# A two-layer hybrid trunk: the borders from token mixer to feed-forward reordered, with the first two up-products of eight pairs put ahead

## The chip, the cores and the metric

The kernel runs on one core of a Trainium2 chip. The metric is the device time of one execution in microseconds (us), the median over the runs shown. PE is TensorE, DVE is VectorE, ACT is ScalarE, POOL is GpSimd, and SP is the engine whose queue issues every DMA of this kernel.

## What is computed

Two DeepNorm layers of width 1024 over 1024 tokens, all in float32. Layer 0 mixes tokens by a dilated window attention, layer 1 by a gated linear recurrence (HGRN2); each is followed by a squared-ReLU feed-forward of width 4096.

```python
for i in range(DEPTH):
    j = i // N_MIXERS
    if i % N_MIXERS == 0:
        y = dilated_attention_mixer(x, attn_w_in[j], attn_w_out[j])
    else:
        y = hgrn2_mixer(x, hgrn_w_in[j], hgrn_w_out[j], hgrn_norm_g[j], lbs[i])
    x = layer_norm(DEEPNORM_ALPHA * x + y, ln_mix_g[i], ln_mix_b[i])
    y = squared_relu_mlp(x, ffn_w_up[i], ffn_w_down[i])
    x = layer_norm(DEEPNORM_ALPHA * x + y, ln_ffn_g[i], ln_ffn_b[i])
```

The attention has three head groups (dilations 1, 4, 16) whose outputs are mixed by a softmax over the groups' log sums; a "unit" below is one pair of heads of one group.

## The kernel before

**Precision.** Every large matrix product is made of three matmuls: an operand is split into a high part (ACT rounds it) and a low part (DVE subtracts, line 125 in `split`), and high x high, high x low, low x high are summed in one bank of PSUM. A "split" below is one ACT and one DVE instruction on 128x512 elements.

**SBUF.** Nearly everything lies in one pool of 46 equal slots of 128x1024 (`U`, `NSLOT`). An instruction that writes a new tile waits until a slot is free. PSUM has eight banks: three "mm", two "s", two "pt", one "o".

**Order.** Each engine works through its own list. Inside the attention's product loop PE's and DVE's lists are as written (`in_order`). Elsewhere the framework lays out the lists when the program is built, by the order of writing and its own estimate of what is ready; at run time every list, SP's DMAs too, is strictly in order, and a waiting instruction holds up all behind it.

**Border 1** (attention to feed-forward, about 1006 to 1220 us). The attention's last pair of units is still in its softmax when the loop of input products ends. `attention` returns what is left of it in `fill`, lists of small pieces: the rotary steps (`ra`, `rb`; a DMA fetches the rotated copy, L446), six core steps for each of the two units (`ca`, `cb`: scores L476, exponentials L490, transposes L500, products L515), the statistics of each unit (`sa`, `sb_`: `combine_tr`, a transpose L541, then a DMA to DRAM and back), and the mixing of the groups (`mx`: `combine` on tiny tiles, six DMAs per part into `frow`, then six `fb` products L597 with DVE multiplications L598 to L602). `oN` is the list of attention outputs, eight tiles of 128 features x 1024 tokens; the first six are spilled to DRAM.

`outproj_ln` projects them. `pr.pre`, called at the last input product, loads and splits the first two (`NPRE`) tiles of `oN`, tokens 0 to 511 (h = 0), with their weights. Then the rest up to six (`NKA`) follow, the second halves of the weights, the second token half (h = 1) of all six, and three residual tiles `z`. **Stage A** accumulates these six features for the token tiles 0 to 5 (two column halves each: twelve half-tiles of 18 matmuls, L170 to L172), and between them pops `fill`, one list at a time: five during the first three half-tiles, one after them, and one after each further half-tile. What `fill` still holds then is written out behind all of stage A. **The finish** (`fin`) adds features 6 and 7 for tiles 0 to 5, all eight for tiles 6 and 7, normalises each tile (`ln_math`: DVE, ACT and one POOL addition, L201) and stores it. `tr(t)` transposes a normalised tile (L210, into the two "pt" banks) and makes the operands of the feed-forward's first product by a scheme with seven instead of eight sub-products (`Fast`): for the second token half this makes the sums T1 to T4, by DVE and POOL in scratch tiles `fs`, ten splits' halves in all (L220, L221).

**The feed-forward** has 16 pairs `p`, each of seven products `i` in 1 to 7. Products 1 and 2 need the first token half alone, the others need T1 to T4. So `seq` puts (p, 1) and (p, 2) of the first four pairs (`NAHEAD`) ahead, then their other five products, then the other pairs in full. After each of the first four products one list of `late` is popped: `tr(6)`, `tr(4)`, `tr(7)`, `tr(5)`. Weights are loaded six products ahead (`load_up`), split three ahead (`split_up`). A pair's `upa` tile holds product 1's copy (L1009) and the square of product 2 (L1012), and stays until its other five products are done.

**Border 2** (HGRN2 to feed-forward, about 2208 to 2370 us) uses the same `outproj_ln` with seven features in stage A and six short lists in `fill`.

Of the kernel before, what the change touches and what calls it, by code (L numbers as in the profile page):

```python
# [9 lines left out]
F32 = mybir.dt.float32  # L10
# [23 lines left out]
NPRE = 2  # L34
SPILL = (6, 5)
NKA = (6, 7)
NAHEAD = 4
# [12 lines left out]
def trunk_kernel(  # L50
# [258 lines left out]
    def attention(pre):  # L309
# [413 lines left out]
        for n in range(len(seq)):  # L723
# [8 lines left out]
            if n == len(seq) - 1:  # L732
                pre(oN)
# [44 lines left out]
    class Out:  # L778
# [10 lines left out]

        def split_w(self, k, dm):  # L790
            hi, lo, raw = self.w[k]
            c = slice(dm * 512, dm * 512 + 512)
            nc.sync.dma_start(raw[:, c], self.w_dram[k][:, c])
            split(raw[:, c], hi[:, c], lo[:, c])
            if dm == 1:
                self.w[k] = (hi, lo)

        def load(self, k, oN, h):
            if k >= SPILL[self.mixer]:
                self.raw[k] = oN[k]  # L800
                return
            if h == 0:
                self.raw[k] = U("onr")
            c = slice(h * 512, h * 512 + 512)
            nc.sync.dma_start(self.raw[k][:, c], oN[k][:, c])
# [14 lines left out]
    def outproj_ln(pr, oN, fill, resid, gB_ap, bB_ap, keep):  # L820
# [9 lines left out]
        for k in range(NPRE, nka):  # L830
# [9 lines left out]
        NA = (6, 6)[pr.mixer]  # L840
# [9 lines left out]
        def stage_a(tiles, n):  # L850
            os = [bank("mm", "pmm") for _ in tiles]
            for ks in [range(nka)] if len(tiles) == 1 else [(k,) for k in range(nka)]:
                for (t, dm), o in zip(tiles, os):
                    rows(o, a, w, t, dm, ks, ks[0] == 0, ks[-1] == nka - 1)
                if len(ks) == 1 and ks[0] in pops:
                    for f in fill.pop(0) if fill else []:
                        f()
            for (t, dm), o in zip(tiles, os):
                c = slice(dm * 512, dm * 512 + 512)
                nc.vector.scalar_tensor_tensor(z[t][:, c], z[t][:, c], ALPHA, o, op0=ALU.mult, op1=ALU.add)  # L860
            for _ in range(n):
                for f in fill.pop(0) if fill else []:
                    f()

        pops = (1, 2, 3, 4, 5, 6) if len(fill) > 12 else (2, 4)
        stage_a([(0, 0), (1, 0), (2, 0)], 1)
        for t in range(NA):
            load_z(max(t, 1) + 1)
            if t == NA - 3:
                for k in range(nka, NK):  # L870
                    pr.load_w(k)
                    pr.split_w(k, 1)
            for dm in range(2):
                if t > 2 or dm:
                    stage_a([(t, dm)], 1)
# [3 lines left out]
        load_z(7)  # L879
        for h in range(2):  # L880
            for k in range(nka, NK):
                pr.raw[k] = oN[k]
                split_k(k, h)
        gB = bcast_rows(gB_ap, "gB")
        bB = bcast_rows(bB_ap, "bB")
        xn = Fast(name + "f")
# [4 lines left out]
        def fin(t, dms=(0, 1)):  # L891
            for dm in dms:
                o = bank("mm", "pmm")
                c = slice(dm * 512, dm * 512 + 512)
                if t < NA:
                    rows(o, a, w, t, dm, range(nka, NK), True, True)
                    nc.vector.tensor_add(z[t][:, c], o, z[t][:, c])
                else:
                    rows(o, a, w, t, dm, range(8), True, True)
# [12 lines left out]
        fin(7, (0,))  # L912
        tr(1)
        fin(4)
        tr(2)
        tr(3)
        fin(7, (1,))
        fin(5)
        return xn, [lambda: tr(6), lambda: tr(4), lambda: tr(7), lambda: tr(5)]


    def ffn(li, xf, late, res, gB_ap, bB_ap, last, pre=None):
# [11 lines left out]
        raw, comb, H = {}, {}, {}  # L934

# [36 lines left out]

        st = [{} for _ in range(NP)]
# [24 lines left out]
        def product_up(n):  # L998
# [9 lines left out]
            if i == 1:  # L1008
                act(p1, o, AF.Copy)  # L1009
            elif i == 2:  # L1010
# [223 lines left out]
        for n in range(len(seq)):  # L1234
            load_up(n + LOADUP)
            product_up(n)
            if late:
                late.pop(0)()
# [263 lines left out]
    hds = [dp.tile([7, NFF // 2, P, 512], F32, name=f"hd{i}") for i in range(2)]  # L1502
    x1d = dp.tile([S, D], F32, name="x1d")
# [3 lines left out]
    oN, fill = attention(pr.pre)  # L1507
# [87 lines left out]
```

## Time and profile before

| | us |
|---|---|
| median of 3 runs (2995.59 to 2996.76) | 2995.66 |
| the profiled execution, its own time | 2997.35 |
| span of its trace | 2995.6 |
| PE busy (95% of the span) | 2832.5 |
| DVE busy (70%) | 2085.3 |
| ACT busy (49%) | 1459.9 |
| POOL busy (15%) | 437.3 |

The profiled execution took 1.75 us more than its span, and stands 1.69 us above the median. PE is busy in 95% of the span, and the chain of work that ended last runs over PE for 75% of it. A busy PE is not yet PE at its peak: a matmul of 512 columns counts 0.39 us though the next one starts 0.23 us after it, and at the lower clock the same work counts as busy for longer. So in the tables by stage the number of instructions is to be read with the busy time.

### The profile page before, as it was taken

To read this page: it belongs to the slowest core of one execution; us is meant where nothing else is said; L and a number is where in the kernel's file an instruction comes from. 1 tells how busy PE (TensorE), PEld (TensorE's weight loads), DVE (VectorE), ACT (ScalarE), POOL (GpSimd) and SP (SyncE) were. 2 spreads that over 40 slices of the span, in tenths; PEclk is the share of its full clock that TensorE was granted. 3 is DMA by queue.
4 is the path that set the end of the run, shared out by engine and by line. 5 is a ranking of instruction groups with operands and counts; after the bars stand their busy time and mean duration, and the time that the engine had idled before them with its cause. 6 is when DMAs were issued, how large, how long until landed. Compare 5 with 4: busy or idle time off the path is not lost.

```text
span 2995.6 us, 40619 instructions
## 1 busy us (share of the span) xinstructions
PE 2832.5 (95%) x14152; PEld 2243.5 (75%) x14152; DVE 2085.3 (70%) x3725; ACT 1459.9 (49%) x3136; POOL 437.3 (15%) x211
## 2 busy tenths in 40 slices
PE   7899999999999878999999998999999899999998
PEld 6677777777677656777778876778877677778876
DVE  7668776786787648766686966564566766678784
ACT  5454555555555445444444535554553544454442
POOL 0112111010111103000051311110101200034300
PEclk9999999999999999999999999999999899999999
DMA  8885777767777512344494733101131344475662
GB/s 340 276 268 185 251 250 240 236 239 251 262 234 263 160 55 102 134 151 150 140 316 122 255 118 130 36 29 57 64 134 61 122 146 143 151 272 184 204 204 74
DMA packets 214717, 525.16 MB, mean 175 GB/s; under 512 B 31600, under 2 KB 45936, under 8 KB 214512
## 3 DMA queue, kind: packets, MB, share of 16 engines
q1 hardware_dynamic: 214512, 522.57, 52.0%
q8 instruction: 111, 1.82, 0.3%
q14 instruction: 94, 0.77, 0.1%
HBM read 400.57 MB, written 96.34 MB: 166 GB/s over the span
## 4 chain that ended last, share of the span: by engine, by line
PE 75%; DMA 10%; DVE 10%; issue 2%; ACT 2%; SPq 1%; POOL 0%; DVEq 0%; ACTq 0%; POOLq 0%
PE pmm L638 6%; PE pmm L637 6%; PE pmm L639 6%; PE pup L1004 5%; PE pup L1006 5%; PE pup L1005 5%; PE pdy L1124 4%; PE pdy L1126 4%; PE pdy L1125 4%; PE pmm L158 3%; PE pmm L159 3%; PE pmm L160 3%; DMA wb<-in_w_up_dram 3%; PE pdx L1125 3%; PE pdx L1126 3%
## 5 line engine op out<-in xcount | busy, mean ns | idle before, releaser
L637 PE MATMUL pmm<-xh,H 128*128 128x512 f32 x1008 | 409.9, 407 | 12.8 <-ACT H L410 7.9
L638 PE MATMUL pmm<-xl,H 128*128 128x512 f32 x1008 | 399.3, 396 | 14.0 <-DMA xl<-xtd 13.2
L639 PE MATMUL pmm<-xh,H 128*128 128x512 f32 x1008 | 398.2, 395 | 1.5 <-DVE H L418 1.5
L448 POOL TENSOR_TENSOR rot<-rot,sinT 128x1024 f32<-128x1024 f32 x48 | 136.5, 2845 | 865.7 <-DMA rot<-e 385.2
L638 PEld LDWEIGHTS pmm<-xl,H 128*128 128x128 f32 x1008 | 192.5, 191 | 54.5 <-DMA xl<-xtd 16.4
L637 PEld LDWEIGHTS pmm<-xh,H 128*128 128x128 f32 x1008 | 192.4, 191 | 53.8 <-ACT H L410 7.9
L639 PEld LDWEIGHTS pmm<-xh,H 128*128 128x128 f32 x1008 | 191.9, 190 | 44.1 <-DVE H L418 2.7
L487 DVE CUSTOM_DVE_ANT_0 p<-s,mask 128x128 f32<-128x128 f32 (+1 forms) x384 | 113.1, 347 | 148.2 <-PE s L476 137.2
L1124 PE MATMUL pdy<-dT,dS 128*128 128x512 f32 x512 | 201.7, 394 | 7.5 <-ACT dS L124 7.5
L490 ACT ACTIVATE p<-p,stats 128x128 f32<-128x128 f32 (+1 forms) x384 | 168.2, 441 | 78.4 <-DVE stats L487 78.2
L1125 PE MATMUL pdy<-dT,dS 128*128 128x512 f32 x512 | 201.1, 393 | 0.0
L1126 PE MATMUL pdy<-dT,dS 128*128 128x512 f32 x512 | 201.1, 393 | 0.0
L125 DVE TENSOR_TENSOR dS<-dr,dS 128x512 fp32r<-128x512 f32 x192 | 167.5, 872 | 18.1 <-ACT dS L124 17.4
L124 ACT ACTIVATE dS<-dr 128x512 fp32r<-128x512 f32 x192 | 120.1, 626 | 121.1 <-DVE dT L125 41.8
L503 ACT ACTIVATE pts<-ppt 128x256 f32<-128x256 f32 (+1 forms) x192 | 85.8, 474 | 150.4 <-PE ppt L500 140.4
L158 PE MATMUL pmm<-f0nh,wh 128*128 128x512 f32 x384 | 153.2, 399 | 0.7 <-ACT wh L124 0.7
L160 PE MATMUL pmm<-f0nh,wl 128*128 128x512 f32 x384 | 149.9, 390 | 0.0
L159 PE MATMUL pmm<-f0nl,wh 128*128 128x512 f32 x384 | 149.7, 390 | 0.0
L1096 POOL TENSOR_TENSOR hold<-hold,dr 128x512 f32<-128x512 f32 x32 | 48.3, 1509 | 630.3 <-DMA hold<-in_w_down_dram 325.4
L1124 PEld LDWEIGHTS pdy<-dT,dS 128*128 128x128 f32 x512 | 97.4, 190 | 28.6 <-ACT dS L124 8.3
L125 DVE TENSOR_TENSOR dT<-dr,dT 128x512 fp32r<-128x512 f32 x128 | 116.0, 920 | 4.1 <-ACT dT L124 3.7
L201 POOL TENSOR_TENSOR z<-z,bB 128x1024 f32<-128x1024 f32 x24 | 63.2, 2640 | 357.7 <-ACT z L200 354.7
(394 smaller groups left out, 7233.6 us busy)
## 6 DMA issues: line engine op xcount, KB each, us to landing
xh<-xtd SPq DMA_DIRECT2D x154, 512.0 KB
xl<-xtd SPq DMA_DIRECT2D x154, 512.0 KB
dr<-hd SPq DMA_DIRECT2D x192, 256.0 KB
dr<-in_w_down_dram SPq DMA_DIRECT2D x160, 256.0 KB
rot<-e SPq DMA_DIRECT2D x192, 128.0 KB
wa<-in_w_up_dram SPq DMA_DIRECT2D x40, 512.0 KB
wa<-in_w_attn_dram SPq DMA_DIRECT2D x36, 512.0 KB
wb<-in_w_attn_dram SPq DMA_DIRECT2D x36, 512.0 KB
```

The costliest lines, as they stand in the source:

```text
L125: nc.vector.tensor_sub(lo, raw, hi.bitcast(F32))
L158: nc.tensor.matmul(o, wh[:, k], xs.h(k), start=k == 0, stop=False)
L159: nc.tensor.matmul(o, wh[:, k], xs.l(k), start=False, stop=False)
L160: nc.tensor.matmul(o, wl[:, k], xs.h(k), start=False, stop=k == NK - 1)
L490: act(p[:, h, :n], p[:, h, :n], AF.Exp, bias=sS[:, 0, h, b:b + 1], scale=-1.0, accum_out=sS[:, 1, h, b:b + 1])
L637: nc.tensor.matmul(o, wh, hi[k // 2][:, c], start=begin and k == 0, stop=False, skip_group_check=True)
L638: nc.tensor.matmul(o, wh, lo[k // 2][:, c], start=False, stop=False, skip_group_check=True)
L639: nc.tensor.matmul(o, wl, hi[k // 2][:, c], start=False, stop=end and k == 3, skip_group_check=True)
L1004: nc.tensor.matmul(o, wh, xf.h(b, k), start=begin and k == 0, stop=False, skip_group_check=True)
L1124: nc.tensor.matmul(o[q], h, T_[:, L], start=begin, stop=False, skip_group_check=True)
L1125: nc.tensor.matmul(o[q], h, T_[:, R], start=False, stop=False, skip_group_check=True)
L1126: nc.tensor.matmul(o[q], l, T_[:, L], start=False, stop=end, skip_group_check=True)
```

## The change

- `attention`: `pr.pre_steps` takes the place of `pr.pre`. It issues the loads of three features (`PREA`) nine products before the end, and makes their six splits one by one after each of the last seven products. `fill` has another order (`mine`): single core steps of the two units in turn, the statistics of each unit with its fifth core step, the mixing from the 16th of 22 lists on.
- `outproj_ln`: stage A covers tiles 0 to 3 alone (eight half-tiles); `tick` pops `fill` evenly after every feature of a half-tile; a feature that comes in meanwhile (k = 6) joins stage A; the loads and splits of the second token half (`second`) come two at a time behind the half-tiles, the rest behind stage A. The finish takes tile 0, 4, 1, 4, 2, 5, 3, 5, 6, 6, 7 with all eight features for tiles 4 to 7. `late` has the four transposes in the order 4, 5, 6, 7, each with two empty places before it.
- `ffn`: `NAHEAD` is 8. Pairs 4 to 7 store product 1's copy to DRAM (`p1d`) and load it again, with the square of product 2, when their other products come near.

```diff
+PREA = 3
+EARLY = (2, 0)
+NAHEAD = 8
+NSTAY = 4
+LATE = 2
...
-            if n == len(seq) - 1:
-                pre(oN)
+            if n == len(seq) - 2 * PREA - 3:
+                early = pre(oN)
+            if n >= len(seq) - 2 * PREA - 1:
+                next(early, None)
...
-        lists = [[ra[0]], [rb[0], rb[1]], [ra[1]], [ca[0], rb[2]], [ca[1], cb[0]]]
-        lists = [done[k:k + 1] + (lists[k] if k < len(lists) else []) for k in range(max(len(done), len(lists)))]
-        lists += [[ca[2 + k], cb[1 + k]] for k in range(4)]
-        lists += [[sa[0], cb[5]], [], [sb_[0]], [], [], [mx[0]], [mx[1]], [mx[2]], [], [], mx[3:6], mx[6:9]]
+        mine = [[ra[0]], [rb[0], rb[1]], [ra[1]], [ca[0], rb[2]], [ca[1]], [cb[0]], [ca[2]], [cb[1]], [ca[3]], [cb[2]],
+                [ca[4], sa[0]], [cb[3]], [ca[5]], [cb[4], sb_[0]], [cb[5]], [mx[0]], [mx[1]], [mx[2]], [],
+                mx[3:5], mx[5:7], mx[7:9]]
+        lists = [done[k:k + 1] + (mine[k] if k < len(mine) else []) for k in range(max(len(done), len(mine)))]
...
+        def pre_steps(self, oN):
+            for k in range(PREA):
+                self.load(k, oN, 0)
+                raw = U("wor")
+                self.w[k] = (None, None, raw)
+                nc.sync.dma_start(raw[:, :512], self.w_dram[k][:, :512])
+
+            def steps():
+                for k in range(PREA):
+                    raw = self.w[k][2]
+                    hi, lo = U("woh", F32R), U("wol", F32R)
+                    self.w[k] = hi, lo, raw
+                    split(raw[:, :512], hi[:, :512], lo[:, :512])
+                    yield
+                    self.split_k(k, 0)
+                    yield
...
-        for k in range(nka):
-            pr.load(k, oN, 1)
-            split_k(k, 1)
...
+        ticks = 3 * nka + 5 * 7
+
+        def tick():
+            count[0] += 1
+            while fill and count[1] * ticks < count[0] * total:
+                for f in fill.pop(0):
+                    f()
+                count[1] += 1
...
+        def second(n):
             for _ in range(n):
-                for f in fill.pop(0) if fill else []:
-                    f()
...
+                if ahead and len(oN) > ahead[0]:
+                    k = ahead.pop(0)
+                    pr.load(k, oN, 1)
+                    split_k(k, 1)
+
+        ks = list(range(nka))
+        stage_a([(0, 0), (1, 0), (2, 0)], ks)
+        for n, (t, dm) in enumerate([(0, 1), (1, 1), (2, 1), (3, 0), (3, 1)]):
...
+            stage_a([(t, dm)], ks)
+            if n >= EARLY[pr.mixer]:
+                second(2)
...
         fin(0)
+        fin(4, (0,))
         fin(1)
-        fin(6, (0,))
+        fin(4, (1,))
         fin(2)
-        fin(6, (1,))
+        fin(5, (0,))
         fin(3)
         tr(0)
-        fin(7, (0,))
+        fin(5, (1,))
         tr(1)
-        fin(4)
         tr(2)
+        fin(6, (0,))
         tr(3)
-        fin(7, (1,))
-        fin(5)
-        return xn, [lambda: tr(6), lambda: tr(4), lambda: tr(7), lambda: tr(5)]
+        fin(6, (1,))
+        fin(7)
+        late = []
+        for t in (4, 5, 6, 7):
+            late += [None] * LATE + [lambda t=t: tr(t)]
+        return xn, late
...
+            if i == 6 and NSTAY <= p < NAHEAD:
+                t = st[p]["a"] = U("upa")
+                nc.sync.dma_start(t[:, L], p1d[li, p])
+                nc.sync.dma_start(t[:, R], hd[0, p])
...
             if i == 1:
                 act(p1, o, AF.Copy)
+                if NSTAY <= p < NAHEAD:
+                    nc.sync.dma_start(p1d[li, p], p1)
```

## Rows read from the trace of the kernel before

**Rows 1.** The page's part 2: TensorE's busy tenths and granted clock in 40 slices.

```profile
PE   7899999999999878999999998999999899999998
PEclk9999999999999999999999999999999899999999
```

**Rows 2.** Busy time by stage: stretch, length, then each engine's busy us (instructions), clock, DMA.

```profile
1006.00:1103.00 97.00, 84.80 (x495) 61.29 (x496) 59.02 (x139) 49.38 (x135) 4.75 (x2) 1.00 0.40 128
1103.00:1128.00 25.00, 9.98 (x38) 6.04 (x35) 12.83 (x26) 2.86 (x7) 0.00 (x0) 0.67 0.05 15
1128.00:1170.00 42.00, 40.70 (x195) 32.76 (x195) 38.26 (x78) 20.28 (x47) 14.62 (x6) 0.99 0.26 97
1170.00:1219.00 49.00, 33.52 (x129) 24.78 (x130) 41.12 (x76) 29.99 (x71) 16.00 (x10) 0.86 0.30 106
1219.00:1274.00 55.00, 54.16 (x237) 43.98 (x236) 41.01 (x67) 24.55 (x43) 0.00 (x0) 1.00 0.46 156
2208.00:2279.00 71.00, 70.39 (x370) 57.34 (x369) 35.80 (x72) 22.51 (x45) 0.00 (x0) 1.00 0.25 82
2279.00:2308.00 29.00, 27.78 (x130) 22.48 (x129) 27.47 (x55) 10.58 (x23) 11.18 (x5) 1.00 0.17 65
2308.00:2368.00 60.00, 44.91 (x173) 33.55 (x172) 51.20 (x99) 38.28 (x92) 19.23 (x12) 0.77 0.34 122
```

**Rows 3.** PE in order of time, border 1: start, duration, operation, idle before it.

```profile
1046.94 0.93 PE L476 MATMUL s<-kT,qT 64*128 64x128 f32 x8 [1.67 <-DVE kT L450]
...
1147.31 1.04 PE L210 MATMUL lnpt<-ident,z 128*128 128x128 f32 x8
```

**Rows 4.** All engines in order of time: the last exponential of the attention.

```profile
1092.41 0.50 ACT L490 ACTIVATE p<-p,stats 128x256 f32<-128x256 f32 x1
```

**Rows 5.** PE in order of time, from the statistics to the finish.

```profile
1103.83 0.28 PE L541 MATMUL mpt<-ident,stats 128*32 128x128 f32 x1
...
1119.83 1.19 PE L597 MATMUL fb<-frow,bsel 128*128 128x512 f32 x2 [13.62 <-DMA frow<-fl]
...
1125.41 0.79 PE L170 MATMUL pmm<-woh,aoh 128*128 128x512 f32 x1 [0.47 <-ACT aoh L124]
```

**Rows 6.** SP's DMA issues in order of time, in the attention's tail.

```profile
1024.68 5.51 SPq L845 DMA_DIRECT2D z<-in_x_dram  x3
...
1030.96 5.62 SPq L446 DMA_DIRECT2D rot<-e  x8
```

**Rows 7.** PE's waits, 1170 to 1220: us in total, times, longest.

```profile
PE lnpt L210 <- DVE fs L288: 5.5, 2, 3.6
PE pup L1004 <- ACT H L124: 5.3, 3, 3.4
```

**Rows 8.** PE's waits, 2279 to 2370.

```profile
PE lnpt L210 <- DVE fs L288: 5.1, 2, 3.1
PE pup L1004 <- ACT H L124: 5.0, 2, 3.4
```

**Rows 9.** PE in order of time: matmuls at the lower clock, then at full clock.

```profile
1216.13 0.63 PE L1006 MATMUL pup<-af21h,H 128*128 128x512 f32 x1
1216.55 0.63 PE L1004 MATMUL pup<-af21h,H 128*128 128x512 f32 x1
...
1218.02 0.39 PE L1005 MATMUL pup<-afT2l,H 128*128 128x512 f32 x1
...
1219.60 0.39 PE L1006 MATMUL pup<-afT2h,H 128*128 128x512 f32 x1
```

**Rows 10.** Stage 1170 to 1219, instructions with the scratch tiles fs alone.

```profile
1170.00:1219.00 49.00, 22.56 (x40) 13.46 (x36) 10.78 (x8) 0.86 0.30 106
```

**Rows 11.** DVE's groups, 1170 to 1219: busy us, mean ns.

```profile
L125 DVE TENSOR_TENSOR H<-wa,H 128x512 fp32r<-128x512 f32 x8 | 5.4, 674 | 0.0
```

**Rows 12.** DVE's groups, 2279 to 2368.

```profile
L125 DVE TENSOR_TENSOR H<-wa,H 128x512 fp32r<-128x512 f32 x8 | 7.6, 949 | 0.0
```

More of the change, by code (lines that the diff above doesn't have):

```diff
@@ L788, in load_w @@
             self.split_w(k, 0)
+        def pre_steps(self, oN):
[13 more added lines that the diff above has]
+                    yield
+            return steps()
         def split_w(self, k, dm):
@@ L801, in load @@
                 return
[L802 to L803 removed]
+            self.raw[k] = U("onr")
             c = slice(h * 512, h * 512 + 512)
@@ L829, in outproj_ln @@
         nka = NKA[pr.mixer]
-        for k in range(NPRE, nka):
+        for k in range((PREA, NPRE)[pr.mixer], nka):
             pr.load(k, oN, 0)
@@ L848, in outproj_ln, with stage_a @@
         load_z(2)
-        def stage_a(tiles, n):
+        parts = {}
+        total = max(len(fill), 1)
+        count = [0, 0]
+        ticks = 3 * nka + 5 * 7
[5 more added lines that the diff above has]
+                count[1] += 1
+        def stage_a(tiles, ks):
             os = [bank("mm", "pmm") for _ in tiles]
-            for ks in [range(nka)] if len(tiles) == 1 else [(k,) for k in range(nka)]:
+            for k in ks:
                 for (t, dm), o in zip(tiles, os):
-                    rows(o, a, w, t, dm, ks, ks[0] == 0, ks[-1] == nka - 1)
-                if len(ks) == 1 and ks[0] in pops:
-                    for f in fill.pop(0) if fill else []:
-                        f()
+                    rows(o, a, w, t, dm, (k,), k == ks[0], k == ks[-1])
+                    tick()
             for (t, dm), o in zip(tiles, os):
@@ L860, in stage_a @@
                 nc.vector.scalar_tensor_tensor(z[t][:, c], z[t][:, c], ALPHA, o, op0=ALU.mult, op1=ALU.add)
+                parts[t, dm] = ks
+        ahead = [k for k in range(NK)]
+        def second(n):
             for _ in range(n):
[L862 to L867, printed above, removed]
-            load_z(max(t, 1) + 1)
[L869 to L875, printed above, removed]
+                if ahead and len(oN) > ahead[0]:
[5 more added lines that the diff above has]
+        for n, (t, dm) in enumerate([(0, 1), (1, 1), (2, 1), (3, 0), (3, 1)]):
+            load_z(max(t, 1) + 1)
+            if n in (1, 3) and len(w) < NK:
+                k = len(w)
+                pr.load_w(k)
+                pr.split_w(k, 1)
+            k = len(ks)
+            if k < 7 and len(oN) > k and k < len(w):
+                pr.raw[k] = oN[k]
+                split_k(k, 0)
+                ks = ks + [k]
+            stage_a([(t, dm)], ks)
+            if n >= EARLY[pr.mixer]:
+                second(2)
+        while len(w) < NK:
+            k = len(w)
+            pr.load_w(k)
+            pr.split_w(k, 1)
         while fill:
@@ L878, in outproj_ln @@
                 f()
[L879 to L883, printed above, removed]
+        for k in range(len(ks), NK):
+            pr.raw[k] = oN[k]
+            split_k(k, 0)
         gB = bcast_rows(gB_ap, "gB")
         bB = bcast_rows(bB_ap, "bB")
+        second(NK)
         xn = Fast(name + "f")
@@ L891, in fin @@
         def fin(t, dms=(0, 1)):
+            load_z(t)
             for dm in dms:
@@ L894, in fin @@
                 c = slice(dm * 512, dm * 512 + 512)
-                if t < NA:
-                    rows(o, a, w, t, dm, range(nka, NK), True, True)
+                old = parts.get((t, dm), [])
+                rows(o, a, w, t, dm, [k for k in range(NK) if k not in old], True, True)
+                if old:
                     nc.vector.tensor_add(z[t][:, c], o, z[t][:, c])
                 else:
-                    rows(o, a, w, t, dm, range(8), True, True)
                     nc.vector.scalar_tensor_tensor(z[t][:, c], z[t][:, c], ALPHA, o, op0=ALU.mult, op1=ALU.add)
@@ L934, in ffn @@
         raw, comb, H = {}, {}, {}
+        st = [{} for _ in range(NP)]
         def key(p, half, i):
@@ L971, in split_up @@
             H[p, i] = parts_of(a22 if i == 4 else comb[p][i], "H")
-        st = [{} for _ in range(NP)]
         def pair_tile(p, name):
@@ L1236, in ffn @@
             product_up(n)
-            if late:
-                late.pop(0)()
+            f = late.pop(0) if late else None
+            if f:
+                f()
             split_up(n + SPLITUP)
@@ L1502, in trunk_kernel @@
     hds = [dp.tile([7, NFF // 2, P, 512], F32, name=f"hd{i}") for i in range(2)]
+    p1d = dp.tile([2, NAHEAD, P, 512], F32, name="p1d")
     x1d = dp.tile([S, D], F32, name="x1d")
@@ L1506, in trunk_kernel @@
     pr = Out(w_attn_out, "a", 0)
-    oN, fill = attention(pr.pre)
+    oN, fill = attention(pr.pre_steps)
     xf, late = outproj_ln(pr, oN, fill, lambda t: x[t * P:(t + 1) * P, :],
```

2 lines of the change are left out of this document (removed).

## The prediction

> **What bounds the kernel now.** I read the page's slices first. PE is full nearly everywhere, and apart from the start the slices that fall below 9 lie at two places, around 1000 to 1200 us and around 2300 to 2370 us: the two borders that the change rewrites [rows 1]. Elsewhere PE's own matmuls set the time, and their number stays. So the question is how much of PE's time at the borders is lost, and the busy time by stage answers it [rows 2]. The price of a matmul comes from PE's list: seven steps from 1218.02 to 1219.60 are 0.226 us each at the full 2.4 GHz, and one step from 1216.13 to 1216.55 is 0.42 us at 1.2 GHz [rows 9]. Eight transposes take 1.04 us [rows 3].
>
> - Attention tail with stage A, 1006 to 1103: PE idle 97.0 - 84.8 = 12.2 us.
> - 1103 to 1128: 38 instructions, 21 of them wide: 21 x 0.226 + about 1.3 for the small ones = 6 us of work in 25, so 19 lost. Of these 13.6 are one wait for the weights of the mixing (frow); the rest runs at a mean clock of 0.67 [rows 2, 5].
> - Border 1's finish and ahead products, 1128 to 1219: 324 instructions; eight tiles were transposed, 64 of the 324, so 260 x 0.226 + 8 x 1.04 = 67 us in 91, 24 lost.
> - Border 2's, 2279 to 2368: 303 instructions, 239 x 0.226 + 8.3 = 62 us in 89, 27 lost. Its stage A (2208 to 2279) loses 0.6 and has nothing to give [rows 2].
>
> In all 82 us, 2.7% of the span, are there to be won. The waits name the cause in the last two stages: transposes wait until DVE has emptied the two banks of the tile before, and products wait for their weight's splits, which stand in the same lists [rows 7, 8]. DVE is busy 79 of 91 us and 79 of 89 us there [rows 2]. PE has too little work of its own to lay beside it: with 96 ahead products it has 67 and 62 us.
>
> **Part 1: the finish with eight pairs ahead.** Stage A now covers eight half-tiles, so matmuls move behind it: at border 1 stage A falls from 216 to 156 matmuls (52 features of half-tiles x 3) and the finish grows from 168 to 228; at border 2 from 252 to 168, and from 132 to 216. Four more pairs add 8 x 12 = 96 ahead products, taken from later. PE's work from the finish to the first T2 product becomes 228 x 0.226 + 8.3 + 192 x 0.226 = 103 us at border 1 and 216 x 0.226 + 8.3 + 43.4 = 100 us at border 2. DVE's grows by eight weight splits of 0.674 us [rows 11] and two late splits of the second token half: 79 + 5.4 + 1.4 = 86 us. PE becomes the longer list at both borders. Within the ahead phase one `tr` falls on three products: PE 3 x 12 x 0.226 + 1.04 = 9.2 us, DVE 22.56/4 = 5.6 us in scratch tiles [rows 10] + 3 x 0.674 = 7.7 us. That fits, with 1.5 us to spare. What remains lost: the entry of (0, 6), whose sums stand behind the last `tr` on DVE (3.4 us, the longest wait of its kind [rows 7, 8]), one or two waits for banks, and a little at the lower clock. I take a third of before, 8 us for each border; bounds are 0 and all that is lost now. **Gain 24 - 8 = 16 and 27 - 8 = 19 us.**
>
> POOL's share: the same weight split takes DVE 0.949 us at border 2 and 0.674 at border 1 [rows 11, 12]. With the eight added ones at 0.949 DVE would have 2.2 us more at each border and stay below PE, so the sum stays. The Trainium skill (GPSIMD Engine Reference, section 1, Specifications) says that POOL shares its SBUF interfaces with DVE and contends with DVE instructions that have two SBUF inputs, which these splits are. It speaks against laying more of them beside POOL's additions, and by it some 4 us of the gain would go; the trace agrees that they stretch (0.949 against 0.674).
>
> **Part 2: the attention's tail.** Three features are split during the last input products, so that PE finds its first operands at once. That adds no work, but six DVE instructions move into the loop's strict order and their loads ahead on SP, and if slots are short there, PE waits. Nothing shows this; were each to hold PE for one split's 0.674 us, it would cost 4 us, and the other way it can win a part of the 12.2 us that 1006 to 1103 loses. I take 0, since DVE and SP have no more to do in sum. Then I follow the chain that ends last, link by link.
>
> - *To the first scores of the last units*, 1046.94, which still wait 1.67 us for their key [rows 3]. The rotary loads behind that key are issued on SP at 1030.96, behind residual loads of 5.51 us from 1024.68 [rows 6] and behind the loads of the second token half. The latter move behind the half-tiles of stage A, with their slots. I take 8 us earlier, half of the 1046.94 - 1030.96 at most.
> - *From there to the last exponential*, 1092.41 [rows 4], 45 us in which stage A and the scores share PE. With 60 matmuls (13.6 us) fewer to stand between I take half of these, 7 us; the other half is ACT's and DVE's own time.
> - *To the transposed statistics*, 1103.83 [rows 5]: 11.4 us of mere queueing, since these pieces are written behind stage A. The new order has each unit's statistics with its fifth core step. I take half, 6 us, since pieces of the other unit now stand between.
> - *From there to the finish*, 1125.41 [rows 5]: 21.6 us of DMAs, tiny tiles and mixing that stay.
>
> So the finish begins at 1125.4 - 21 = 1104. PE's work up to there is 119.4 us less the 12 and 18 lost, 89, and without the 60 matmuls 76. That leaves 98 - 76 = 22 us lost, of which the half-tile of token tile 4, written second in the finish with seven of its eight features ready, can fill 21 x 0.226 = 4.7. Lost 17, against 31: **gain 14 us**. Bounds: -9 (the chain ends where it did: 4.7 - 13.6) and +26 (5 us left).
>
> **Part 3: what is added.** In each layer four stores and eight loads of 256 KB and four weight loads of 512 KB, 5 MB. They lie where DMA is 0.30 to 0.46 busy [rows 2], beside PE's full list, and come six products ahead: 0. Without that cover, a reload late by 3.4 us, the longest wait for a split [rows 7], for each of four pairs would cost 14 us a layer. The store of product 1 makes SP wait for ACT's copy; behind it stand weight loads due six products later (16 us), so nobody waits. Slots: four `upa` are held as before, and the other four are given back. Border 2's stage A shrinks by 84 x 0.226 = 19 us from 71, and its pieces, 52 us with PE full, keep their cover: 0.
>
> **Sum:** 14 + 16 + 19 = 49 us. The profiled execution (2997.35 for a span of 2995.6) becomes 2948.4; the median stands 1.7 below it: **2947 us**.
>
> **The rivals.**
> 1. *The tail's chain ends where it did.* For it: SP's in-order list and the DMAs to DRAM and back are untouched, and DVE is busy 59 of 97 us there. Against it: 11 us of the chain are plain queueing. Tail -9, borders +35: 2996 - 26 = 2970.
> 2. *The borders stay bound by the exchange between ACT, DVE and POOL*, PE's waits only move to the later transposes: borders 0 to 5, tail 14: about 2980. For it: the waits are for single DVE and ACT results; against it: PE's longer list.
> 3. *Slower: the ahead phase runs at 1.2 GHz.* The granted clock was 0.86 and 0.77 in these stages [rows 2], always behind a wait. If one `tr` with three weight splits takes DVE and ACT over the 9.2 us that PE has beside it, every third product waits and the clock falls in each group. Then the eight added products cost 96 x (0.42 - 0.226) = 19 us more in each layer, nothing of the 24 and 27 comes back, and the tail gives 14: 2996 + 38 - 14 = 3020. The Trainium skill (TensorE: Matmul & The Clock Gate, section HAM oscillation — how this bites in real kernels) tells of kernels in which each wait throws the clock back to half rate; the trace shows this at both borders, at a mean of 0.86 and 0.77. Against it: 7.7 of 9.2 us.
>
> **Numbers.** Forecast 0.55 with its own range 2928 to 2966; better, the tail's stall gone too (2925), 0.06; rival 1 0.17; rival 2 0.12; rival 3 0.07; the change moves stalls about and nothing comes of it (2990 to 3000) 0.03. The 8 in 10 range reaches from 2922 to 2982. A measurement of this kernel tells about 0.2%, 6 us, from no change: faster 0.87, within it 0.05 (the last case and parts of rivals 2 and 3), slower 0.08.
>
> **What would show it.** Right: PE idle under 10 us between the finish and the first T2 product in both layers, clock 1.00 in nearly all of it; statistics transposed within a few us of the last exponential; the wait for frow well under 13.6 us. Wrong: `lnpt` or `pup` waits of over 20 us at a border (rival 2), a clock of 0.5 to 0.8 through the ahead products (rival 3), a finish that begins later than 1120 us (rival 1), `upa` reloads that release PE.

## The result, and the profile after

The changed kernel took 2945.01 us (median of 4) beside 2996.21 us for the kernel before on the same chip: ratio 0.9822 with an interval of 0.9802 to 0.9842. One of the four executions, at 4928.45 us, had its matmuls 0.40 to 0.45 us apart from start to end (0.23 in the others); it counts in this median but not in the ratio, and the profile below is of a second set of the same kernel. That set gave 2941.28 us (2938.02 to 2941.97) beside 2995.33: ratio 0.9815 [0.980, 0.983], 54 us. The forecast was 2947.

The page's part 2 of the changed kernel, TensorE's busy tenths and granted clock in 40 slices:

```profile
PE   7899999999899989999999999999999999999998
PEclk9999999999999989999999999999999999999999
```

Of the "878" around 1000 to 1200 us [rows 1] one 8 is left, in the tail, which now also has the one 8 of the clock; the clock's 8 at the second border is gone. Busy time by stage of the changed kernel (columns as in [rows 2]): the second half of border 1, the tail as a whole, border 1 from the finish to the first T2 product (the first that needs the second token half), then border 2's end of stage A and its finish with the ahead products:

```profile
1156.00:1204.00 48.00, 46.43 (x215) 36.93 (x215) 38.93 (x71) 34.06 (x81) 13.68 (x9) 1.00 0.41 143
1006.00:1100.00 94.00, 82.04 (x454) 57.21 (x452) 59.76 (x145) 44.91 (x128) 5.64 (x2) 0.92 0.32 95
1100.00:1204.00 104.00, 99.54 (x450) 79.60 (x451) 88.17 (x163) 57.43 (x131) 31.59 (x16) 0.98 0.35 127
2180.00:2230.00 50.00, 49.98 (x267) 40.43 (x266) 31.31 (x67) 16.53 (x34) 0.00 (x0) 1.00 0.27 87
2230.00:2281.00 51.00, 49.19 (x232) 40.26 (x231) 41.69 (x80) 22.52 (x48) 16.75 (x7) 1.00 0.31 120
2281.00:2329.00 48.00, 46.43 (x216) 36.90 (x214) 38.70 (x71) 33.96 (x80) 13.68 (x9) 1.00 0.41 141
```

"Lost" is, as in the prediction, the length of a stage less the time that its matmuls and transposes take at full clock: of the 450 instructions at border 1, 64 are transposes, so 386 x 0.226 + 8.3 = 95.5 us of work in 104, 8.5 lost (24 before). Border 2 has 448 in 99 us: 384 x 0.226 + 8.3 = 95.1, 3.9 lost (27 before). The granted clock is 1.00 in the ahead products (1156 to 1204, 2281 to 2329), where it was 0.86 and 0.77 [rows 2]. PE's longest waits at border 1 (us in total, times, longest):

```profile
PE lnpt L214 <- issue: 1.5, 2, 0.9
PE pmm L174 <- DVE z L947: 1.0, 1, 1.0
PE pup L1058 <- ACT H L128: 0.9, 1, 0.9
```

The transposes' wait for the sums in `fs`, 5.5 and 5.1 us before [rows 7, 8], is not among them; what is left of the wait for ACT's half of a split is 0.9 instead of 5.3.

**The tail.** I measure it from the last input product to the last `fb`, because the moment at which the attention gets there differs from run to run. Five of the kernels below have the same code up to the finish (the changed one, four pairs, no spacing, all pairs through DRAM, twelve pairs); their tails take 96.0, 95.3, 95.0, 95.1 and 97.1 us, so a difference of up to 2 us tells nothing. The changed kernel's PE in order of time (start, duration, operation, idle before):

```profile
1003.15 0.39 PE L643 MATMUL pmm<-xh,H 128*128 128x512 f32 x1
...
1041.92 0.93 PE L480 MATMUL s<-kT,qT 64*128 64x128 f32 x8 [0.25 <-DVE kT L454]
...
1075.10 0.28 PE L545 MATMUL mpt<-ident,stats 128*32 128x128 f32 x1
...
1094.79 1.20 PE L601 MATMUL fb<-frow,bsel 128*128 128x512 f32 x2 [2.13 <-DMA frow<-fl]
...
1100.38 0.80 PE L174 MATMUL pmm<-woh,aoh 128*128 128x512 f32 x1 [0.47 <-ACT aoh L128]
```

and its last exponential on ACT:

```profile
1071.97 0.49 ACT L494 ACTIVATE p<-p,stats 128x256 f32<-128x256 f32 x1
```

Before, the last input product began at 1005.74:

```profile
1005.74 0.39 PE L639 MATMUL pmm<-xh,H 128*128 128x512 f32 x1
```

From it to the last `fb` were 118.4 us (1124.15); now they are 96.0 (1099.11). Output-projection matmuls up to the finish fell from 3 x 75 = 225 to 179 (the `pmm<-woh,aoh` group and its two sisters: 60, 60, 59):

```profile
L174 PE MATMUL pmm<-woh,aoh 128*128 128x512 f32 x60 | 26.3, 444 | 7.8 <-ACT aoh L128 4.0 <-DVE z L891 2.0 <-DVE vT L676 1.3
L175 PE MATMUL pmm<-wol,aoh 128*128 128x512 f32 x60 | 25.3, 422 | 0.0
L176 PE MATMUL pmm<-woh,aol 128*128 128x512 f32 x59 | 24.9, 424 | 0.8 <-DVE aol L129 0.8
```

So of 22.4 us, 46 x 0.226 = 10.4 are work moved behind the tail, and 12.0 are won. (By the forecast's measure, the time lost up to the finish, it is the same: 12 of its 31 are gone, 19 are left.) The wait for frow fell from 13.62 [rows 5] to 2.13. **In sum** 12.0 + 15.5 + 23.1 = 50.6 us. The stages of before reach 6 us past the first T2 product, those after the change end at it; with 6 us added after the change too, 9.3 and 5.2 us are lost, and the sum is 48. The two profiled spans differ by 59.4: 5 of it is the distance of the two profiled executions from the medians of their sets, 2.6 (which may be part of the 5) arises before the last input product, well within the scatter of that moment (999.66 to 1013.99 us, see the last section), and the rest lies in no stage that I assigned.

A measure that needs no choice of stages: the `pdx` products of the feed-forwards, the first of this group in layer 0, the last in layer 1 (count, lowest/mean/highest ns, first to last start), of the kernel before, then of the changed one:

```profile
L1124 PE MATMUL pdx<-dT,dS x256: 388/389/500, 1512.2 to 2839.4; 128*128 128x512 f32 x128
```

```profile
L1180 PE MATMUL pdx<-dT,dS x256: 388/389/504, 1479.9 to 2780.6; 128*128 128x512 f32 x128
```

From the last input product to the first `pdx` the time fell from 506.4 to 476.7 (29.7: tail and border 1), from there to the last from 1327.2 to 1300.7 (26.5: border 2 and all between).

### The profile page after: what moved, and what is told of

Read it like the earlier page. It is cut to its first block, busy times and chain, and to the rows that moved or that the text cites. A ratio compares the mean times of both kernels' runs of the same rounds, so it can differ in the third digit from the quotient of the medians.

```text
span 4926.6 us, 40675 instructions
## 1 busy us (share of the span) xinstructions
PE 4897.6 (99%) x14152; PEld 2933.5 (60%) x14152; DVE 2092.1 (42%) x3717; ACT 1466.5 (30%) x3136; POOL 405.1 (8%) x211
## 4 chain that ended last, share of the span: by engine, by line
PE 99%; DVE 0%; ACT 0%; DMA 0%; issue 0%; SPq 0%; DVEq 0%; ACTq 0%
PE pmm L641 10%; PE pmm L643 10%; PE pmm L642 10%; PE pup L1060 7%; PE pup L1058 7%; PE pup L1059 7%; PE pdy L1181 4%; PE pdy L1182 4%; PE pdy L1180 4%; PE pmm L162 3%; PE pmm L164 3%; PE pmm L163 3%; PE pdx L1182 3%; PE pdx L1181 3%; PE pdx L1180 3%; PE s L480 3%
## 5 line engine op out<-in xcount | busy, mean ns | idle before, releaser
L641 PE MATMUL pmm<-xh,H 128*128 128x512 f32 x1008 | 699.9, 694 | 8.2 <-ACT H L414 8.2
L643 PE MATMUL pmm<-xh,H 128*128 128x512 f32 x1008 | 681.8, 676 | 0.0
L642 PE MATMUL pmm<-xl,H 128*128 128x512 f32 x1008 | 681.5, 676 | 0.0
L643 PEld LDWEIGHTS pmm<-xh,H 128*128 128x128 f32 x1008 | 300.9, 298 | 172.5 <-issue 155.1
L641 PEld LDWEIGHTS pmm<-xh,H 128*128 128x128 f32 x1008 | 297.0, 295 | 170.1 <-issue 145.4
L642 PEld LDWEIGHTS pmm<-xl,H 128*128 128x128 f32 x1008 | 297.2, 295 | 150.4 <-issue 140.3
L1182 PE MATMUL pdy<-dT,dS 128*128 128x512 f32 x512 | 295.3, 577 | 0.0
L1181 PE MATMUL pdy<-dT,dS 128*128 128x512 f32 x512 | 295.2, 577 | 0.0
L1180 PE MATMUL pdy<-dT,dS 128*128 128x512 f32 x512 | 294.1, 574 | 0.0
L162 PE MATMUL pmm<-f0nh,wh 128*128 128x512 f32 x384 | 222.9, 580 | 0.3 <-ACT wh L128 0.3
L163 PE MATMUL pmm<-f0nl,wh 128*128 128x512 f32 x384 | 220.7, 575 | 0.0
L164 PE MATMUL pmm<-f0nh,wl 128*128 128x512 f32 x384 | 220.6, 575 | 0.0
L1182 PEld LDWEIGHTS pdy<-dT,dS 128*128 128x128 f32 x512 | 111.9, 219 | 85.3 <-issue 50.6
L1180 PEld LDWEIGHTS pdy<-dT,dS 128*128 128x128 f32 x512 | 112.1, 219 | 84.4 <-issue 47.9
L1181 PEld LDWEIGHTS pdy<-dT,dS 128*128 128x128 f32 x512 | 111.1, 217 | 85.3 <-issue 50.3
L1181 PE MATMUL pdx<-dT,dS 128*128 128x512 f32 x256 | 147.9, 578 | 0.9 <-DVE dT L129 0.9
```

The source lines that it names most:

```text
L162: nc.tensor.matmul(o, wh[:, k], xs.h(k), start=k == 0, stop=False)
L163: nc.tensor.matmul(o, wh[:, k], xs.l(k), start=False, stop=False)
L164: nc.tensor.matmul(o, wl[:, k], xs.h(k), start=False, stop=k == NK - 1)
L641: nc.tensor.matmul(o, wh, hi[k // 2][:, c], start=begin and k == 0, stop=False, skip_group_check=True)
L642: nc.tensor.matmul(o, wh, lo[k // 2][:, c], start=False, stop=False, skip_group_check=True)
L643: nc.tensor.matmul(o, wl, hi[k // 2][:, c], start=False, stop=end and k == 3, skip_group_check=True)
```

## The experiments

All ratios are to the kernel before on the same chip in the same set; 0.1% is 3 us. `lost` at a border is always reckoned as above, from the instructions of the stage.

**The change again**, unaltered, as the yardstick.

> The changed kernel itself, unaltered, to have its trace. Every theory: 2945 us within 6. Theory 1 (PE now has work of its own beside DVE's in the borders): PE loses 8 to 10 us between the finish and the first T2 product in each layer, at a clock near 1.00 (24 and 27 before), and about 17 us in the attention's tail (31 before). Rival (the tail gave most of it): the borders still lose over 15 us each and the tail under 5.

Measured 2941.28 us, 0.9815 [0.980, 0.983]; its profile is the one above.

**Without the four added pairs.**

```diff
-NAHEAD = 8
+NAHEAD = 4
-LATE = 2
+LATE = 1
```

(Four pairs have eight products ahead, so only one empty place fits before each transpose: two things differ from the changed kernel, the pairs and the spacing.)

> The changed kernel with four pairs ahead instead of eight (the four transposes then after every second of the eight ahead products). Theory 1 (number of products beside DVE's work): PE has 81 us of work beside 80 us of DVE's, so about half of the borders' gain goes: 2962 us (2955 to 2972). Rival (the gain is in the order, first token half normalised first and transposes spread): within 6 us of the changed kernel, 2939 to 2951.

Measured 2979.2 us, 0.9943 [0.9929, 0.9958]: a miss by 17 us. From the last input product to the first `pdx` 12.3 us are won, about what its tail gives alone (95.3 us to the last `fb`; 23.1 less than before, 10.4 of it moved work). Busy time of its two borders:

```profile
1103.00:1204.00 101.00, 86.11 (x367) 67.81 (x368) 81.68 (x156) 50.36 (x116) 32.35 (x16) 0.91 0.29 106
2255.00:2351.00 96.00, 81.61 (x361) 65.00 (x360) 74.59 (x144) 49.24 (x114) 31.18 (x16) 0.93 0.31 111
```

PE has 303 x 0.226 + 8.3 = 76.8 us of work at border 1 and 75.4 at border 2, DVE 81.7 and 74.6: lists of about the same length. Yet 24 and 21 us are lost (24 and 27 before). PE's waits at border 1 of this kernel:

```profile
PE lnpt L214 <- DVE fs L292: 4.9, 2, 4.8
PE pup L1058 <- ACT upa L1063: 3.8, 1, 3.8
PE pup L1058 <- ACT afT2h L224: 2.9, 1, 2.9
```

The old wait for `fs` is back, with waits for ACT beside it. The longer finish with four pairs is worth nothing at border 1 and 6 us at border 2.

**The pairs alone**: the kernel before with the feed-forward's part of the change.

```diff
-NAHEAD = 4
+NAHEAD = 8
+NSTAY = 4
...
+            if i == 6 and NSTAY <= p < NAHEAD:
+                t = st[p]["a"] = U("upa")
+                nc.sync.dma_start(t[:, L], p1d[li, p])
+                nc.sync.dma_start(t[:, R], hd[0, p])
...
+                if NSTAY <= p < NAHEAD:
+                    nc.sync.dma_start(p1d[li, p], p1)
```

> The kernel before with the feed-forward's part of the change alone: eight pairs ahead, product 1 of four of them stored and reloaded; tail, finish and late transposes as before. Theory 1: the four transposes still come after the first four products, so their waits for banks stay (5 us a layer), but twelve more products follow them before T1 to T4 are needed: 20 us won, 2976 (2966 to 2984). Rival (order): under 6 us won, over 2990.

Measured 2982.88 us, 0.9962 [0.995, 0.9974], 11 us, half of what theory 1 wanted. Its two borders, and PE's waits at the first:

```profile
1124.00:1232.00 108.00, 93.40 (x407) 72.69 (x405) 84.67 (x161) 59.10 (x133) 31.53 (x16) 0.94 0.31 111
2273.00:2373.00 100.00, 84.72 (x381) 66.05 (x381) 81.26 (x158) 57.90 (x130) 31.45 (x16) 0.97 0.33 119
```

```profile
PE lnpt L211 <- DVE fs L289: 5.5, 2, 3.6
PE pup L1010 <- DVE H L126: 3.2, 3, 2.1
PE pup L1008 <- ACT upa L1013: 2.5, 1, 2.5
```

Work 343 x 0.226 + 8.3 = 85.8 us in 108: 22 lost at border 1, hardly fewer than the 24 before, though PE now has as much to do as DVE (84.7). At border 2 it is 20 (27 before). The wait for `fs` is exactly as long as in [rows 7]. The transposes still come after each of the first four products, so more work behind them helps little at border 1 and 7 us at border 2.

**The pairs, with the transposes spaced** (two empty places before each, in the old order).

```diff
-        return xn, [lambda: tr(6), lambda: tr(4), lambda: tr(7), lambda: tr(5)]
+        late = []
+        for t in (6, 4, 7, 5):
+            late += [None] * 2 + [lambda t=t: tr(t)]
+        return xn, late
```

> The kernel before (its tail, its finish order) with eight pairs ahead and the four late transposes spaced as in the change, two empty places before each. Theory 2 (neither part alone is enough: without more pairs PE lacks work, and with the transposes at the first four products PE stands in front of banks that DVE has not emptied, with the work behind it in its list): the waits of the run with pairs alone go, some 20 us won against it, 2960 (2954 to 2970); what is left to the changed kernel is the tail. Rival (the finish with the first token half normalised first is what lets PE run on): stays near the run with pairs alone, 2976 to 2988.

Measured 2968.86 us, 0.9908 [0.9878, 0.9937]: 28 us where the pairs alone gave 11. Its two borders, and what is left of PE's waits at the first:

```profile
1126.00:1226.00 100.00, 92.34 (x403) 72.62 (x402) 82.83 (x159) 56.91 (x130) 32.09 (x16) 0.94 0.33 119
2260.00:2360.00 100.00, 91.36 (x410) 72.52 (x408) 82.15 (x158) 56.71 (x130) 31.66 (x16) 0.97 0.33 119
```

```profile
PE pup L1011 <- ACT H L125: 3.4, 2, 3.1
PE pup L1013 <- DVE H L126: 2.9, 2, 2.2
PE lnpt L211 <- issue: 0.7, 1, 0.7
```

84.9 us of work in 100 at border 1: 15 lost instead of 22, and no transpose waits for `fs` there. At border 2 13.5 are lost instead of 20. What remains are waits for splits.

**The change without the spacing.**

```diff
-LATE = 2
+LATE = 0
```

> The changed kernel with the transposes of the second token half at the first four products, no empty places. Theory 2: PE stands in front of the banks again, 8 to 14 us a layer: 2963 (2956 to 2972). Rival (spacing does not matter once there are eight pairs and the new finish): within 5 us of the changed kernel, 2936 to 2946.

Measured 2959.54 us, 0.9876 [0.9848, 0.9905]: 0.6%, some 18 us, of the gain are gone. Both borders, and PE's longest wait at the first (4.9 at the second):

```profile
1096.00:1209.00 113.00, 102.57 (x450) 81.38 (x451) 87.08 (x164) 58.92 (x131) 32.35 (x16) 0.95 0.32 115
2235.00:2345.00 110.00, 99.01 (x437) 78.80 (x437) 79.91 (x148) 58.21 (x129) 31.58 (x16) 0.94 0.32 118
```

```profile
PE lnpt L214 <- DVE fs L292: 4.7, 2, 3.3
```

PE has the very same 386 matmuls and 64 transposes as in the changed kernel, and a list 8 us longer than DVE's; still 17.5 us are lost at border 1 (8.5 with the spacing) and 17.4 at border 2 (3.9). So a longer list on PE is not enough: it must stand between the transposes. The spacing in turn needs the pairs, since twelve products are the room for four transposes with two empty places each; spacing with four pairs and the old finish was not run.

**The old order of the attention's pieces**, with all else as changed.

```diff
-        mine = [[ra[0]], [rb[0], rb[1]], [ra[1]], [ca[0], rb[2]], [ca[1]], [cb[0]], [ca[2]], [cb[1]], [ca[3]], [cb[2]],
...
+        lists += [[ca[2 + k], cb[1 + k]] for k in range(4)]
+        lists += [[sa[0], cb[5]], [], [sb_[0]], [], [], [mx[0]], [mx[1]], [mx[2]], [], [], mx[3:6], mx[6:9]]
```

> The changed kernel with the old order of the attention's last pieces (26 lists, statistics with and behind the last core step), still popped evenly over stage A. Theory 1 (the chain of scores, statistics and mixing sets the tail's end): statistics come some 6 to 10 us later after the last exponential, and the end moves with them: 2953 (2948 to 2962). Rival (the tail was won by the shorter stage A and the later loads of the second half): 2945 within 4.

Measured 2946.07 us, 0.9831 [0.9815, 0.9846], not distinguishable from the change. From the last input product to the last `fb` it takes 97.0 us, against 96.0 with the new order and 118.4 before. Its last exponential on ACT, and PE's transpose of the statistics after it:

```profile
1082.48 0.49 ACT L494 ACTIVATE p<-p,stats 128x256 f32<-128x256 f32 x1
```

```profile
1087.83 0.28 PE L545 MATMUL mpt<-ident,stats 128*32 128x128 f32 x1
```

So the tail's gain is not the order's: what this kernel shares with the changed one brings nearly all of it. That is the shorter stage A, the even popping by `tick`, the early splits and the later loads of the second token half. The last two are taken back one by one below, for 1 to 3 us each; the first two were not taken apart.

**Four moves in the tail.** Loads and splits of the second token half back ahead of stage A at border 1:

```diff
+        first = nka if pr.mixer == 0 else 0
+        for k in range(first):
+            pr.load(k, oN, 1)
+            split_k(k, 1)
...
-        ahead = [k for k in range(NK)]
+        ahead = [k for k in range(first, NK)]
```

> The changed kernel with the loads and splits of the attention's second token half put back ahead of stage A. Theory 1 (they stood ahead of the rotary loads on SP and held slots): the rotary loads are issued 6 to 10 us later and the finish with them: 2948 (2944 to 2955). Rival (SP waits for the earlier unit's mixing there anyway, 13 us, and the loads fit in behind it): within 3 us of the changed kernel.

Measured 2944.22 us, 0.9830 [0.9801, 0.9859]. The last rotary steps on POOL begin 32.1 us after the last input product instead of 27.3, the last `fb` comes after 98.2 us (95.0 to 97.1 in the five kernels with the change's tail): a link 4.8 us later costs 1 to 3 us at the end, and the median does not tell it from the change.

The early splits taken back:

```diff
-            if n == len(seq) - 2 * PREA - 3:
-                early = pre(oN)
-            if n >= len(seq) - 2 * PREA - 1:
-                next(early, None)
+            if n == len(seq) - 1:
+                pre(oN)
...
-    oN, fill = attention(pr.pre_steps)
+    oN, fill = attention(pr.pre)
```

> The changed kernel with the old start of the projection: two features loaded and split at the last input product, instead of three over the last products. Theory (the early splits save PE's first waits, and the chain through scores, statistics and mixing sets the end anyway): 2942 (2940 to 2947). Rival (the early start is a main part of the tail's gain): 2949 or more; or it costs, by slots and DVE's strict order: 2938 or less.

Measured 2938.32 us, 0.9802 [0.9776, 0.9829]. The first scores come 41.6 us after the last input product, as late as before the change (41.2; 38.8 with it), but the tail takes 98.4 us, only 1 to 3 more than with the change. In the whole time no worth of the early splits can be measured.

The residual loads behind the rotary loads on SP. In the changed kernel SP first stands 13.2 us for the softmax of the unit before, whose mixing DMAs are next in its list, and then issues residual loads ahead of the last rotary loads (SP's waits from 995 to 1045, then its issues in order of time):

```profile
SPq L592 <- ACT p L494: 13.2, 1, 13.2
SPq L450 <- DMA z<-in_x_dram: 4.5, 3, 1.8
```

```profile
1018.39 1.29 SPq L865 DMA_DIRECT2D z<-in_x_dram  x3
...
1021.05 9.64 SPq L450 DMA_DIRECT2D rot<-e  x8
```

The edit, and the issues after it:

```diff
-        load_z(2)
...
             for k in ks:
+                if len(z) < 3 and k == 3:
+                    load_z(2)
```

> The changed kernel with the first three residual loads issued half way through the first three half-tiles, so behind the rotary loads on SP. Theory 1: the rotary copies land 4 to 8 us earlier, the scores and the finish too: 2936 (2932 to 2939). Rival: the rotary loads stand behind the mixing's six small loads, and the chain keeps its time: 2938 to 2944.

```profile
1023.17 5.70 SPq L450 DMA_DIRECT2D rot<-e  x8
1028.97 1.50 SPq L865 DMA_DIRECT2D z<-in_x_dram  x3
```

Measured 2942.0 us, 0.9817 [0.979, 0.9844]: nothing won. The rotary issue takes 5.70 us instead of 9.64 and POOL's rotary steps begin 22.2 us after the last input product instead of 27.3, the first scores 30.2 us after it instead of 38.8, but the tail takes 95.2 us, which the scatter of 95.0 to 97.1 does not tell from the change's. The next links swallow the 8.5 us.

More work in the tail, to fill PE's waits (token tile 4 in stage A at border 1):

```diff
-EARLY = (2, 0)
+EARLY = (0, 0)
...
+        more = [(4, 0), (4, 1)] if pr.mixer == 0 else []
+        for n, (t, dm) in enumerate([(0, 1), (1, 1), (2, 1), (3, 0), (3, 1)] + more):
```

> The changed kernel with both half-tiles of token tile 4 added to the end of border 1's stage A, behind the attention's last pieces, and the second token half loaded from the first half-tile on. Theory 1 (PE idles some 14 us in the tail for lack of ready work while the mixing's DMAs run; 42 matmuls, 9.5 us, can be laid there): 2934 (2929 to 2938). Rival (PE's list already holds tile 4's rows there, and the earlier splits of the second half only crowd DVE, ACT and SP in the chain): 2941 to 2950.

Measured 2943.78 us, 0.9819 [0.9796, 0.9842]: nothing won, though the waits for split attention outputs between 1005 and 1106 us fell from 4.5 us to this:

```profile
PE pmm L174 <- ACT aoh L128: 0.4, 1, 0.4
```

Its tail is as long (95.6 us) with 25 matmuls more in it, but its border 1, with these 25 fewer, is as long too:

```profile
1106.00:1209.00 103.00, 94.38 (x424) 74.07 (x424) 87.15 (x162) 57.23 (x130) 31.08 (x16) 0.98 0.35 126
```

Work 360 x 0.226 + 8.3 = 89.7 us in 103: 13 lost instead of 8.5. So PE's own work is not the whole of what sets border 1's length; in the finish's first 24 us (1106 to 1130) DVE is busy 23.7.

**The added DMAs doubled**: all eight pairs go through DRAM.

```diff
-NSTAY = 4
+NSTAY = 0
```

> The changed kernel with product 1's copy stored and reloaded for all eight pairs instead of four: the added DMAs doubled. Theory (they lie beside PE's full list): 2941 within 4. Rival (SP's waiting stores delay the weight loads, or reloads come late): 3.4 us for each of four pairs, 2950 to 2970.

Measured 2942.59 us, 0.9823 [0.9793, 0.9854]: no cost that can be measured.

**Twelve pairs ahead.**

```diff
-NAHEAD = 8
+NAHEAD = 12
```

> The changed kernel with twelve pairs ahead, four more stored and reloaded. Theory 2 (with eight pairs PE's list is already the longer one): nothing more is won, and four more reloads and weight loads a layer cost little: 2941 (2937 to 2947). Rival (each further pair hides more): 2935 or less.

Measured 2937.48 us, 0.9802 [0.9779, 0.9826], within the change's interval. Its border 1 has 485 matmuls and 64 transposes, 117.9 us of work in 127: 9 lost, as with eight. Four transposes spaced by two places use twelve products, and eight pairs have sixteen. No version was clearly faster than the changed kernel.

## Why the prediction was right

The forecast of 49 us stands beside 53 by the first ratio, 54 by the medians of the second set and 48 to 51 by the stages; rivals 1 (2970), 2 (2980) and 3 (3020) fell. Point by point:

- **Borders: right in size, incomplete in the reason.** 8 us were to remain lost at each; 8.5 and 3.9 did. I credited PE's longer list and used the spacing only to see that a transpose fits beside three products (9.2 us against 7.7). The runs give the spacing more weight (lost at border 1, at border 2): before 24 and 27; the new finish with four pairs 24 and 21; the pairs alone 22 and 20; pairs and new finish without spacing 17.5 and 17.4; the pairs spaced with the old finish 15 and 13.5; all together 8.5 and 3.9. So the spacing is worth 7 us a border with the old finish and 9 and 13.5 with the new one. The new finish is worth nothing at border 1 with four pairs, and 6.5 and 9.6 us with eight spaced. In the whole time the new stage A and finish with four pairs give 17 us (12 of them in the tail), the pairs spaced 28, all 55; that some 10 us come only from having both agrees with the stages but lies within the intervals. Rival 2's picture, single results of DVE and ACT waited for, is what every kernel without the two empty places shows, and in part the spaced one with the old finish; it fell by spacing and finish together, not by the sum of the lists.
- **A miscount that cost nothing.** I had 228 matmuls in border 1's finish and 192 ahead. The profile has 205 and 180 up to the first T2 product. Stage A has its 156, but 23 of the finish's matmuls run before the last `fb`. The forecast let 21 of them (the first half-tile of token tile 4) fill the tail, and yet counted them at the border too. The last ahead product stands behind the first T2 products. PE's work was 95 us, not 103. The 23, and 9 such matmuls that ran there before, are also why the tail shed 46 matmuls and not 60.
- **Two rows misread, at no cost.** The slices [rows 1] have an 8 in two more places, the 25th slice (1797 to 1872 us) and the last. And the 3.4 us that I put down to sums on DVE at the entry of (0, 6) are by their row [rows 7] a wait for ACT's half of a weight split.
- **Tail: the sum right by luck, its links wrong.** The finish was forecast for 1104 us and began at 1100.4, 2.6 of that from an earlier attention. First scores came 2.4 us earlier by the last input product, not 8 (41.2 to 38.8). SP did begin to issue the rotary loads 7.3 us earlier (17.9 after the last input product, 25.2 before). But the issue took 9.64 us instead of 5.62 [rows 6], since 4.5 of it waited for the residual loads, and POOL's steps began 4.9 earlier; I had priced the start of the issue and not its end. From the scores to the last exponential 15.4 us went (45.5 to 30.1), where I took 7, the link that was off by most. From there to the statistics 8.3 went (11.4 to 3.1), for 6. From the statistics to the finish 3.7 came (21.6 to 25.3), for 0: 2.7 of it pass before DVE's first instruction on the tiny tiles (7.0 us after the transpose, 4.3 before), because DVE first stands for the last half-tile of stage A, which is ahead of them in its list:

```profile
1081.46 0.69 DVE L891 SCALAR_TENSOR_TENSOR z<-z,pmm 128x512 f32<-128x512 f32 x1 [3.16 <-PE pmm L176]
```

  The sum is 22.4 for 21, because the errors of the links cancel; a first link 8.5 us earlier moved the end by nothing that can be told (the run with the residual loads later), so the links do not simply add. As a gain 14 were forecast and 12.0 measured. The reason that I gave for the earlier statistics, the new order of the pieces, is mostly refuted: with the old order that link is 5.4 us (1082.48 to 1087.83), so 6 of the 8.3 come without it.
- **Early splits 0, added DMAs 0, border 2's shorter stage A 0:** all three held (the early splits taken back, the DMAs doubled, and PE busy 49.98 of 50 us at the end of stage A).
- **POOL.** The weight split takes DVE 0.872 us on the mean of 13 at border 1 (1156 to 1204), and the same at border 2 (2281 to 2329, shown), between the 0.674 and 0.949 of [rows 11, 12]:

```profile
L129 DVE TENSOR_TENSOR H<-wa,H 128x512 fp32r<-128x512 f32 x13 | 11.0, 872 | 1.5 <-ACT H L128 1.4
```

  These means mislead: eleven of the 13 take 0.67 to 0.69 us, and two, at 1161.92 and 1195.16, take 2.48 and 1.37 us. Each of the two lies beside one addition on POOL. The longer one with its addition, and then the single long one of the eight behind the 0.949 before (the others take 0.65 to 0.68):

```profile
1161.92 2.48 DVE L129 TENSOR_TENSOR H<-wa,H 128x512 fp32r<-128x512 f32 x1 [0.87 <-ACT H L128]
1161.44 2.39 POOL L205 TENSOR_TENSOR z<-z,bB 128x1024 f32<-128x1024 f32 x1 [6.89 <-ACT z L204]
```

```profile
2322.20 2.88 DVE L125 TENSOR_TENSOR H<-wa,H 128x512 fp32r<-128x512 f32 x1
2321.66 2.87 POOL L201 TENSOR_TENSOR z<-z,bB 128x1024 f32<-128x1024 f32 x1 [4.99 <-ACT z L200]
```

  So the splits do not stretch by a third all over: these three each end 0.5 to 0.6 us after POOL's addition does, and others beside an addition are not held (0.67 us at 1182.44, beside the addition of 1182.30 to 1184.27). The Trainium skill (GPSIMD Engine Reference, section 1, Specifications) has POOL contend with such two-input DVE instructions; the trace agrees for these few. The loss forecast for border 1 was met all the same, so the 4 us that I gave it did not go.
- **The clock.** The granted clock in the stage of the four-pair kernel's border 1 has a mean of 0.91, but part of that time PE stood idle anyway. Of its wide matmuls 34 ran at the lower clock (0.63 us long in the profile, a step of 0.42 us instead of 0.226 [rows 9]): 34 x 0.19 = 6.6 us of the 24 lost. Without spacing they are 23, 4.5 us of 17.5, and in the changed kernel 10, 1.9 us of 8.5. So about a quarter of each loss is the clock, nearly all the rest the waits themselves. Rival 3's place, the ahead products, ran at 1.00.

**What stays open:** which of the shorter stage A and the even popping makes the tail's gain, and where the 3 to 6 us between the stages' sum and the medians lie.

## What to carry to other kernels

Adding up each engine's work tells whether two lists *can* overlap; whether they do was decided here as much by the spacing in the lists: lay one costly exchange (here a transpose with its sums) on as much independent work as it takes, and find that work first. Test the parts of such a change alone and together, since a part may look worth nothing until the others are there (the new finish at border 1). In a chain through several engines ask for every link what else the waiting queue holds, and do not add up links: a move that brought the first scores 8.5 us earlier did not end the chain earlier by more than its scatter.

## What was not expected

- Attention code that differs in nothing before its last input product reaches it at 999.66 us in one kernel (no spacing) and at 1013.99 in another (old order of pieces). The waits there that differ are those for one load; from 0 to 990 us, of the first kernel and then of the second:

```profile
PE pmm L642 <- DMA xl<-xtd: 9.4, 6, 4.7
```

```profile
PE pmm L642 <- DMA xl<-xtd: 17.0, 6, 4.3
```

  They hold 7.6 of the 14 us. The kernel before alone spread from 2987.84 to 3004.70 within one set. So for gains under 10 us here a stage measured from a near event (the tail from its last input product) tells more than the time of the whole.
- Two lists of 77 and 82 us, exchanging work in a fixed order, took 101 us (four pairs). Lists of 95 and 87 took 113 us without the spacing and, as 95 and 88, 104 with it.
